# Attention scores for two query tiles at a time, their 64-row rotary products issued in turn on either half of the array's rows

## The chip, the cores and the metric

The kernel runs on one core of a Trainium2 chip. The metric is the device time of one execution in microseconds (us). Engines are named as the profile names them: PE is TensorE's matmul stream, PEld its weight loads, DVE is VectorE, ACT ScalarE, POOL GpSimd, SP SyncE.

## The reference

Two layers of a latent-token backbone, batch 1, 1024 tokens of width 1024, and 256 context tokens. Layer 0 mixes by multi-head latent attention, layer 1 by a Fourier transform. The change is in layer 0's attention. Cut to it:

```
NH, QK_NOPE, QK_ROPE, V_DIM = 8, 128, 64, 128          # 1024 queries, 256 + 1024 keys
k_all = concat([k_ctx, k_lat], axis=1)                 # per head: 128 plain + 64 rotary columns
scale = 1 / sqrt(QK_NOPE + QK_ROPE)
s = einsum('bqhd,bkhd->bhqk', q, k_all) * scale        # the 64 rotary columns of k are shared by all heads
p = softmax(s, axis=-1)
o = einsum('bhqk,bkhd->bqhd', p, v_all)                # then o * silu(gate), output product, residual
```

The low-rank key is used as it stands: the head's key matrix is folded into the query, so that the 128 plain columns of the keys are the same latent vector for all heads, and the head's value matrix is applied behind the sum over keys.

## The kernel before, in words

**Number format.** A float32 product is made from two rounded halves of each factor (`split`: a high part by ACT, the rest by DVE), as high times high, high times low and low times high, each one pass of PE. The probabilities and the latent values are held as two float16 halves each.

**Where the attention lies.** The profiled execution does layer 0's norms, projections and gate until 204.8 us, the attention from 204.8 to 565 us, and layer 0's output product and all of layer 1 behind it. The attention is 8 heads of 8 query tiles of 128; a pair is two neighbouring tiles, 32 in all.

**One tile of scores** (`scores`, L581 to L590) is 128 queries by 1280 keys, in three banks of PSUM, in column pieces of 512, 512 and 256. Five passes go into it. Three are for the plain part: `nkh` with `qh`, `nkl` with `qh`, `nkh` with `ql` (n: keys, q: folded query, h and l: high and low). Two are for the rotary part. `A` holds a head's rotary query, high in rows 0 to 63 and low in rows 64 to 127; `B1` holds the rotary key's low part in rows 0 to 63 and its high part in rows 64 to 127. So `A` with `B1` (128 rows) gives high times low and low times high at once, and high times high is left: `A[0:64]` with `B2` (the key's high part), a product of only 64 rows. That makes 15 matmuls a tile, three of them with 64 rows. Tiles use banks 0 to 2 and 3 to 5 alternately. Banks 6 and 7 are taken in turn by everything else in the attention.

**Behind the scores.** `expo` (L592): DVE takes the row maximum from PSUM (L594), ACT the exponential from PSUM into `p32` with its row sum (L596). This frees the tile's three banks. `quant` (L599): DVE takes the reciprocal and scales it (L600, L602), ACT writes the float16 high part `phi` (L605), DVE the low part `plo` (L607), and each is transposed by a DMA into `PT`. `pv` (L610) is 30 float16 matmuls of 256 columns for a pair, in one bank; `pv_out` splits it into `O` (ACT L90, DVE L91). After each second pair `values` (L619) is three products of `O` with the value matrix in one bank, and DVE multiplies them into `gate` (L623).

**Preparing the next head.** `prep_q` (L559) makes one half of the folded query of head h + 1: the head's weights are split (`wqh`, `wql`), six products go into one bank, and ACT and DVE write `qh` and `ql` from it. `prep_pe` (L570), for two heads at a time and so only during odd heads, transposes the rotary queries into one bank (four transposes) and splits them into two `A`.

**Order.** The loop (L662 to L702) runs over the 64 tiles. `quant` lags the scores by one tile, the product with the values by two pairs (`LAG`), half a pair beside each tile. The order of the instructions on each engine is not written by hand here: a scheduler places them, so `pv`, `values`, `prep_q` and `prep_pe` stand between the passes of the scores. The order of PE is fixed by hand only ahead of the attention.

**Ahead of the attention**, `finish_p2` (L393) transposes a tile of the keys and writes `nkh`, `nkl`, `B1` and `B2`.

Of the kernel before, what the change touches and what calls it, by code (L numbers as in the profile page):

```python
# [17 lines left out]
P = 128  # L18
D = 1024
T = 1024  # L20
# [24 lines left out]
def hybrid_kernel(tc, io, out, dbg=None):  # L45
# [47 lines left out]
    # all of PSUM, handed out bank by bank  # L93
# [69 lines left out]
    # both vectors for a quarter of the array's columns, and the sum over the quarters  # L163
# [98 lines left out]
    def c_mm(k, uc):  # L262
        # one bank holds both: the first write clears it for the two of them
        for t in range(2):
            sl = slice(t * P, (t + 1) * P)
            w = wih[:, k, 256:448], wil[:, k, 256:448]
            for i, (l, r) in enumerate(hl(uc[0][:, sl], uc[1][:, sl], *w)):
                mm(pb[:, 4, t * 192:t * 192 + 192], l, r, start=k + t + i == 0, stop=k == 7 and i == 2, skip_group_check=True)
# [79 lines left out]
    B2 = keyp.tile([64, NC + T], F32R, name="B2")  # L348
# [44 lines left out]
    def finish_p2(nat, t, ctx, kt):  # L393
        tb = bank(7, 1)
        for i in range(2 if ctx else 0, 4):
            nc.tensor.transpose(tb[:, i * P:(i + 1) * P], nat[:, i * P:(i + 1) * P], ident)
        if not ctx:
            dst = slice(t * P, (t + 1) * P)
            split(cqh[:, :, dst], cql[:, :, dst], tb[:, 0:256].rearrange("p (e c) -> p e c", e=2))
        ks = slice(kt * P, (kt + 1) * P)  # L400
        split(nkh[:, ks], nkl[:, ks], tb[:, 256:384])
        act(B1[64:128, ks], tb[64:128, 384:512], AF.Copy)
        split(B2[:, ks], B1[0:64, ks], tb[0:64, 384:512])
# [9 lines left out]
    # a tile's transposes follow two others' arithmetic  # L413
# [21 lines left out]
    # the weights of the rotary queries take a turn among the chunks  # L435
# [33 lines left out]
    def mod_rows(pair):  # L469
        # sums over the partitions, each half of a third in a quarter of the array's columns  # L470
        b = bank(1, 5, 6, 7)
        for c in range(4):
            a = thirds[pair][c // 2][:, (c % 2) * 512:(c % 2) * 512 + 512]
            mm(b[32 * c:32 * c + 32, :], ones[:, 0:32], a, start=True, stop=True)
        row = qmp.tile([P, 512], F32, name="row", tag="row", bufs=1)
        act(row, b, AF.Copy)
        nc.sync.dma_start(modd[2 * pair:2 * pair + 2, :].rearrange("a (h c) -> (a h) c", h=2), row[0:P:32, :])
# [92 lines left out]
    def prep_pe(h, bl):  # L570
        cs = slice(bl * 512, (bl + 1) * 512)
        tb = bank(6, 7)
        for i in range(4):
            nc.tensor.transpose(tb[:, i * P:(i + 1) * P], qpe[:, bl * 4 + i, h * 64:h * 64 + P], ident)  # L574
        for d in range(2):
            A, src = As[(h + d) % 4], tb[64 * d:64 * d + 64, :]
            split(A[0:64, cs], A[64:128, cs], src, scale=SCALE)
# [3 lines left out]
    def scores(h, t):  # L581
        qh, ql = q1[h % 2]
        A1 = As[h % 4]
        s = banks(3, 0, 3).rearrange("p a b -> p (a b)")
        q = slice(t * P, (t + 1) * P)
        passes = [(qh[:, q], nkh), (qh[:, q], nkl), (ql[:, q], nkh), (A1[:, q], B1), (A1[0:64, q], B2)]
        for i, (l, r) in enumerate(passes):
            for a, z in KS:
                mm(s[:, a:z], l, r[:, a:z], start=i == 0, stop=i == 4)  # L589
        return s[:, 0:1280]  # L590
# [39 lines left out]
    s = scores(0, 0)  # L630
    e = expo(s)
# [10 lines left out]
    steps = [(h, t) for h in range(NH) for t in range(8)]  # L642
    PTs, Os, PVb = {}, {}, {}
    prev = None
# [3 lines left out]
    def pv_step(i, half):  # L648
        h, pr = i // 4, i % 4
        if half == 0:  # L650
            PVb[i] = bank(6, 7)
            if pr % 2 == 0:
                Os[h, pr // 2] = [atp.tile([P, 512], F32R, name="O", tag=f"O{j}", bufs=2) for j in range(2)]
            pv(PVb[i], range(0, 5), PTs[i])
        else:
            b = PVb.pop(i)
            pv(b, range(5, 10), PTs.pop(i))
            pv_out(b, pr, Os[h, pr // 2])
            if pr % 2 == 1:
                values(h, pr // 2, Os.pop((h, pr // 2)))  # L660

    for i, (h, t) in enumerate(steps):  # L662
        if t % 2 == 0:
            PTs[i // 2] = [atp.tile([P, 2, NKT, P], F16, name="PT", tag=f"PT{j}", bufs=2) for j in range(2)]
        if i > 0:
            s = scores(h, t)
            e = expo(s)
        if prev is not None:
            quant(*prev)
        prev = (*e, PTs[i // 2], t % 2)  # L670
        if i in (1, 3):
            wvr = atp.tile([P, 4, P], F32, name="wvr", tag="wvr", bufs=1)
            hs = slice(2 * i - 2, 2 * i + 2)
            nc.gpsimd.dma_start(wvr, io["wv"][:, hs, :])
            split(wvh[:, hs, :], wvl[:, hs, :], wvr, scale=gkva)
        if i == 3:
            for n, v in ((2, sh1), (3, scr)):
                nc.gpsimd.dma_start(v, modd[n].rearrange("(k p) -> p k", p=P))
        if i == 16:
            stt(sc1, scr, 1.0, ng[:, 8:16], ALU.add, ALU.mult)  # L680
        if i // 2 >= LAG:
            pv_step(i // 2 - LAG, t % 2)
        if h + 1 < NH:
            if t in (2, 4):
                prep_q(h + 1, t // 2 - 1)
            if h % 2 and t in (3, 5):
                prep_pe(h + 1, t // 4)
        elif t == 0:
# [7 lines left out]
        elif t in (2, 3, 4):  # L696
            k = t - 2
            for i_ in range(2):
                split(*wo0[k][i_], wraw[k][:, i_ * 512:(i_ + 1) * 512], gtt)
        if h == NH - 1 and t in (5, 6, 7):  # L700
            k = t - 1
            nc.gpsimd.dma_start(wraw[k % 4], io["w_out0"][k * P:(k + 1) * P, :])  # L702
# [24 lines left out]
    quant(*prev)  # L727
    for i in (30, 31):
        for half in range(2):
            pv_step(i, half)  # L730
# [168 lines left out]
    # the sum's own token: its products' partial sums are added over the partitions  # L899
# [12 lines left out]
    # odd parts take the place of the input, their weights that of its second half  # L912
# [7 lines left out]
    # projections onto the even halves; the gate's weights make room for them  # L920
# [39 lines left out]
    # the last product's weights: half of the rows early, half in place of the odd parts' weights  # L960
# [292 lines left out]
```

## Time and profile before

| what | value |
|---|---|
| device time, 3 runs | 922.14, 923.68, 926.61 us (median 923.68) |
| span of the profiled execution | 919.9 us, 3.8 below the median of the runs |
| PE busy | 887.2 us, 96% of the span |
| PEld, DVE, ACT, POOL busy | 719.6, 596.9, 407.3, 274.1 us |
| attention, first score product to last product with the values | about 204.8 to 565.1 us |

A busy share near 100% on PE alone does not tell that PE is at its peak, since a matmul's end is modelled; the distance from one matmul's start to the next one's is what a product costs. The other engines' idle time costs nothing as long as PE does not wait for them.

### The profile page before, as it was taken

Reading aid. Unit: us, or ns where it says so; the run is one execution under the profiler, and the core shown is the slowest. Engines: PE = TensorE matmul, PEld = TensorE weight load, DVE = VectorE, ACT = ScalarE, POOL = GpSimd, SP = SyncE. Lnnn points to the kernel's source line nnn. Section 1 sums busy time; section 2 is a strip of 40 time slices with the busy share of each in tenths; the row PEclk is TensorE's granted clock in tenths of the full one; section 3 lists DMA queues with packets and bytes.
Section 4 is the critical chain, followed back from the end, with each engine's and each line's share of the span. In section 5 each row is a group of like instructions: output and inputs, shape, how many; then the busy total and the mean of one; then the engine's idle time right before and its main releaser. Section 6 shows DMA issues by size and latency. Waiting matters only on the chain. (4 is left out here: it accounts for less than half of the span.)

```text
span 919.9 us, 13239 instructions
## 1 busy us (share of the span) xinstructions
PE 887.2 (96%) x4963; PEld 719.6 (78%) x4963; DVE 596.9 (65%) x1058; ACT 407.3 (44%) x697; POOL 274.1 (30%) x242
## 2 busy tenths in 40 slices
PE   4999999989999999999999999999999999999996
PEld 2878877857777777777777777888888889998885
DVE  4366885765777677777677675365288746297654
ACT  4465511136665655655566654223343236332211
POOL 2544362210000000000000504765276635356311
PEclk9999999999999999999999999999999999999999
DMA  8921456723886666566799976312133425642321
GB/s 337 335 87 46 157 165 229 259 86 67 149 138 116 122 120 115 108 122 132 143 167 157 170 138 180 152 69 92 47 137 115 149 92 193 207 132 89 104 87 51
DMA packets 200744, 127.90 MB, mean 139 GB/s; under 512 B 171931, under 2 KB 175708, under 8 KB 200424
## 3 DMA queue, kind: packets, MB, share of 16 engines
q1 hardware_dynamic: 198632, 119.10, 50.0%
q0 software_dynamic: 2048, 7.95, 2.9%
q8 instruction: 39, 0.64, 0.3%
q14 instruction: 25, 0.20, 0.1%
HBM read 72.51 MB, written 12.57 MB: 92 GB/s over the span
## 5 line engine op out<-in xcount | busy, mean ns | idle before, releaser
L596 ACT ACTIVATE p<-pb,mx 128x1280 f32<-128x1280 f32 x64 | 84.9, 1326 | 93.4 <-DVE mx L594 63.9
L594 DVE TENSOR_REDUCE mx<-pb 128x1 f32<-128x1280 f32 x64 | 95.1, 1487 | 38.6 <-PE pb L589 38.5
L607 DVE SCALAR_TENSOR_TENSOR plo<-p,mx,phi 128x1280 f16<-128x1280 f32 x64 | 99.6, 1566 | 25.8 <-ACT phi L605 24.7
L80 PE MATMUL pb<-PT,n16h 128*128 128x256 f16 x640 | 109.3, 274 | 0.0
L589 PE MATMUL pb<-B,A 128*128 128x512 f32 (+3 forms) x384 | 99.5, 374 | 0.0
L605 ACT ACTIVATE phi<-p,mx 128x1280 f16<-128x1280 f32 x64 | 85.9, 1357 | 21.8 <-DMA PT<-phi 10.6
L80 PE MATMUL pb<-PT,n16l 128*128 128x256 f16 x320 | 87.3, 273 | 0.0
L589 PEld LDWEIGHTS pb<-B,A 128*128 128x128 f32 (+1 forms) x384 | 62.4, 186 | 26.1 <-issue 17.5
L695 POOL DMA_DIRECT2D qpe<-w_out x4 | 2.1, 534 | 244.1 <-PE pb L574 244.1
L80 PEld LDWEIGHTS <-n16h 128*128 128x128 f16 x640 | 59.2, 98 | 19.5 <-issue 12.9
L88 POOL TENSOR_TENSOR ol<-gate,oh 128x512 fp32r<-128x512 f32 (+4 forms) x30 | 43.4, 1460 | 64.6 <-ACT oh L87 64.6
L464 DVE SCALAR_TENSOR_TENSOR aacc<-aw,actc,aacc 128x512 f32<-128x512 f32 x49 | 44.3, 922 | 17.7 <-DMA aacc<-b_ada 9.8
L589 PE MATMUL pb<-nkh,qh 128*128 128x512 f32 (+1 forms) x192 | 53.4, 384 | 0.1
L80 PE MATMUL pb<-wl,oh 128*128 128x512 f32 x128 | 50.1, 393 | 1.5 <-DVE wl L88 1.4
L80 PE MATMUL pb<-uh,gh 128*128 128x512 f32 x128 | 50.4, 394 | 0.0
L80 PE MATMUL pb<-ul,gh 128*128 128x512 f32 x128 | 50.1, 392 | 0.0
L80 PE MATMUL pb<-uh,gl 128*128 128x512 f32 x128 | 50.0, 391 | 0.0
L80 PE MATMUL pb<-wh,ol 128*128 128x512 f32 x128 | 49.8, 391 | 0.0
L80 PE MATMUL pb<-wh,oh 128*128 128x512 f32 x128 | 49.0, 397 | 0.0
L589 PE MATMUL pb<-nkl,qh 128*128 128x512 f32 (+1 forms) x192 | 47.9, 357 | 0.0
L589 PE MATMUL pb<-nkh,ql 128*128 128x512 f32 (+1 forms) x192 | 47.8, 357 | 0.0
L87 ACT ACTIVATE oh<-gate 128x512 fp32r<-128x512 f32 (+4 forms) x38 | 19.6, 556 | 54.4 <-PE pb L80 43.9
(327 smaller groups left out, 2204.6 us busy)
## 6 DMA issues: line engine op xcount, KB each, us to landing
aw<-w_ada SPq DMA_DIRECT2D x49, 256.0 KB, 3.4
wada<-wada SPq DMA_DIRECT2D x16, 512.0 KB, 9.1
gr<-wg SPq DMA_DIRECT2D x14, 512.0 KB, 4.1
xn<-x SPq DMA_DIRECT2D x8, 512.0 KB, 5.4
xt<-x SPq DMA_DIRECT2D x8, 512.0 KB, 7.4
h1d<-xt SPq DMA_DIRECT2D x8, 512.0 KB, 2.6
wz<-wz SPq DMA_DIRECT2D x8, 512.0 KB, 4.1
ht<-h1d SPq DMA_DIRECT2D x8, 512.0 KB, 5.4
```

What stands on the lines that cost most here:

```text
L80: mm(ps, l, r, start=start and i == 0, stop=stop and i == n - 1)
L87: act(hi, src, AF.Copy)
L88: eng(lo, src, f32(hi), ALU.subtract)
L464: op = stt(a[:, cs], w, actc[:, k, 0:1], a[:, cs], ALU.mult, ALU.add)
L589: mm(s[:, a:z], l, r[:, a:z], start=i == 0, stop=i == 4)
L594: nc.vector.tensor_reduce(mx[:, 0:1], s, axis=AX, op=ALU.max, negate=True)
L596: act(p32, s, AF.Exp, bias=mx[:, 0:1], accum_out=mx[:, 1:2])
L605: act(hi, p32, AF.Copy, scale=r)
L607: stt(lo, p32, r, hi, ALU.mult, ALU.subtract)
L695: nc.gpsimd.dma_start(wraw[k], io["w_out0"][k * P:(k + 1) * P, :])
```

## The change

The loop runs over the 32 pairs. `scores(h, pr)` makes both tiles of a pair, the even tile in banks 0 to 2, the odd one in banks 3 to 5. First come four passes with 128 rows for the even tile, then four for the odd one. The last of the four is `A` with `B1` for the even tile and `A` with `B2` for the odd one: for odd tiles `A` now holds its low part in rows 0 to 63 and its high part below, and `B2` has 128 rows, the key's high part above and its low part below. So either kind of tile still has one 128-row pass for its two small rotary products, and one product of 64 rows (high times high) left over. Then, for each of the three column pieces, the even tile's 64-row product runs on rows 0 to 63 of the array and the odd tile's on rows 64 to 127, one after the other in program order. The number of matmuls is the same, 30 a pair.

```diff
-    B2 = keyp.tile([64, NC + T], F32R, name="B2")
+    B2 = keyp.tile([P, NC + T], F32R, name="B2")
...
-        act(B1[64:128, ks], tb[64:128, 384:512], AF.Copy)
-        split(B2[:, ks], B1[0:64, ks], tb[0:64, 384:512])
+        split(B1[64:128, ks], B2[64:128, ks], tb[64:128, 384:512])
+        split(B2[0:64, ks], B1[0:64, ks], tb[0:64, 384:512])
...
+        pairs = lambda v, e: v.rearrange("p (a e c) -> p a e c", e=2, c=P)[:, :, e, :]
         for d in range(2):
             A, src = As[(h + d) % 4], tb[64 * d:64 * d + 64, :]
-            split(A[0:64, cs], A[64:128, cs], src, scale=SCALE)
+            for e in range(2):
+                top, low = (pairs(A[64 * x:64 * x + 64, cs], e) for x in range(2))
+                split(*((low, top) if e else (top, low)), pairs(src, e), scale=SCALE)
...
-    def scores(h, t):
+    def scores(h, pr):
         qh, ql = q1[h % 2]
         A1 = As[h % 4]
-        s = banks(3, 0, 3).rearrange("p a b -> p (a b)")
-        q = slice(t * P, (t + 1) * P)
-        passes = [(qh[:, q], nkh), (qh[:, q], nkl), (ql[:, q], nkh), (A1[:, q], B1), (A1[0:64, q], B2)]
-        for i, (l, r) in enumerate(passes):
-            for a, z in KS:
-                mm(s[:, a:z], l, r[:, a:z], start=i == 0, stop=i == 4)
-        return s[:, 0:1280]
+        s = [pb[:, 3 * e:3 * e + 3, :].rearrange("p a b -> p (a b)") for e in range(2)]
+        q = [slice((2 * pr + e) * P, (2 * pr + e + 1) * P) for e in range(2)]
+        for e in range(2):
+            passes = [(qh, nkh), (qh, nkl), (ql, nkh), (A1, B2 if e else B1)]
+            for i, (l, r) in enumerate(passes):
+                for a, z in KS:
+                    mm(s[e][:, a:z], l[:, q[e]], r[:, a:z], start=i == 0, stop=False)
+        for a, z in KS:
+            for e in range(2):
+                x = slice(64 * e, 64 * e + 64)
+                mm(s[e][:, a:z], A1[x, q[e]], (B1 if e else B2)[x, a:z], start=False, stop=True)
+        return [v[:, 0:1280] for v in s]
...
+    order = tc.manual_schedule(engines={mybir.EngineType.PE})
+    order.__enter__()
+    for i in range(4 * NH):
+        h, pr = i // 4, i % 4
...
+            ss = scores(h, pr)
+            es = [expo(s) for s in ss]
+        for e in range(2):
+            quant(*es[e], PTs[i], e)
...
+        if i > LAG:
+            values_step(i - LAG - 1)
         if h + 1 < NH:
-            if t in (2, 4):
-                prep_q(h + 1, t // 2 - 1)
-            if h % 2 and t in (3, 5):
-                prep_pe(h + 1, t // 4)
+            if pr in (1, 2):
+                prep_q(h + 1, pr - 1)
+                if h % 2:
+                    prep_pe(h + 1, pr - 1)
...
+        if i >= LAG:
+            pv_step(i - LAG)
```

Three things come with it. PE's order through the whole loop is now fixed by hand: the pair's scores; `values` of the third pair before, where due; `prep_q` (heads 0 to 6, pairs 1 and 2 of a head); `prep_pe` (odd heads, the same pairs); and last the whole product with the values of the pair two before. There is no second set of banks for the scores: a pair takes all six. And `A` is written in four pieces of 64 by 2 by 128 instead of two of 64 by 512, the keys' rotary part in two splits instead of a copy and a split (ten more DVE operations of 64 by 128 ahead of the attention).

On PE, during head 1, beside the first `prep_pe`, there stood before (qh_2033 and ql_2034 are the head's folded query, B_773 is `B1`, B_774 `B2`):

```order
L589 MATMUL pb<-nkh,qh_2033 128x512 x2
L589 MATMUL pb<-nkh,qh_2033 128x256
L574 MATMUL pb<-ident,qpe 128x128 x4
L589 MATMUL pb<-nkl,qh_2033 128x512 x2
L589 MATMUL pb<-nkl,qh_2033 128x256
L589 MATMUL pb<-nkh,ql_2034 128x512 x2
L589 MATMUL pb<-nkh,ql_2034 128x256
L589 MATMUL pb<-B_773,A_1924 128x512 x2
L589 MATMUL pb<-B_773,A_1924 128x256
L589 MATMUL pb<-B_774,A_1924 128x512 x2
L589 MATMUL pb<-B_774,A_1924 128x256
L589 MATMUL pb<-nkh,qh_2033 128x512 x2
```

With the change, in head 1's pair 2, from the odd tile's last 128-row pass on (L600 are the 64-row products, L575 the transposes of `prep_pe`, O with gh and gl `values`, cq with wq `prep_q`, PT with n16 the product with the values):

```order
L596 MATMUL pb<-B_774,A_1934 128x256
L600 MATMUL pb<-B_774,A_1934 128x512
L600 MATMUL pb<-B_773,A_1934 128x512
L600 MATMUL pb<-B_774,A_1934 128x512
L600 MATMUL pb<-B_773,A_1934 128x512
L600 MATMUL pb<-B_774,A_1934 128x256
L600 MATMUL pb<-B_773,A_1934 128x256
L80 MATMUL pb<-O,gh_781 128x512 x2
L80 MATMUL pb<-O,gl_782 128x512
L80 MATMUL pb<-cqh,wqh 128x512
...
L575 MATMUL pb<-ident,qpe 128x128 x4
L80 LDWEIGHTS n16h
```

The three 64-row products of each tile have become six in a row for a pair, and everything that uses banks 6 and 7 has moved from between the passes to behind the pair's scores, in one order: `values`, `prep_q`, `prep_pe`, product with the values. Counted through the whole program, 70 stretches of 64-row products stood in PE's order before, 36 of them followed by a float32 product and 34 by a float16 one; now there are 32, 23 and 9 of each kind.

On DVE, around the same two halves of `prep_q` and `prep_pe` in head 1, there stood before:

```order
L91 SCALAR_TENSOR_TENSOR ql_1922<-pb,gks,qh_1921 128x512
L594 TENSOR_REDUCE mx<-pb 128x1
L607 SCALAR_TENSOR_TENSOR plo<-p_2442,mx,phi 128x1280
L600 RECIPROCAL mx<-mx 128x1
L602 TENSOR_SCALAR mx<-mx 128x1
L91 SCALAR_TENSOR_TENSOR O<-pb,O 128x256
L91 SCALAR_TENSOR_TENSOR A_2035<-pb,A_2035 64x512
L594 TENSOR_REDUCE mx<-pb 128x1
L607 SCALAR_TENSOR_TENSOR plo<-p_2494,mx,phi 128x1280
L91 SCALAR_TENSOR_TENSOR A_2036<-pb,A_2036 64x512
L600 RECIPROCAL mx<-mx 128x1
L623 TENSOR_TENSOR gate<-pb,gate 128x512
```

With the change, in pair 2 of head 1 (L605 is the maximum, L634 the product with `gate`, L611 and L613 the reciprocal and its scale):

```order
L605 TENSOR_REDUCE mx<-pb 128x1 x2
L634 TENSOR_TENSOR gate<-pb,gate 128x512
L611 RECIPROCAL mx<-mx 128x1
L88 TENSOR_TENSOR wql<-wqk,wqh 128x256
L613 TENSOR_SCALAR mx<-mx 128x1
L91 SCALAR_TENSOR_TENSOR ql_1932<-pb,gks,qh_1931 128x512
L611 RECIPROCAL mx<-mx 128x1
L613 TENSOR_SCALAR mx<-mx 128x1
L618 SCALAR_TENSOR_TENSOR plo<-p_2595,mx,phi 128x1280
L91 SCALAR_TENSOR_TENSOR A_2072<-pb,A_2072 64x2x128
```

Both maxima of a pair stand one behind the other now, and the operations that free banks 6 and 7 (`gate`, `ql`, `A`, `O`) stand behind them. In pair 1 of an odd head `ql` comes directly behind the two maxima.

## Rows read from the trace of the kernel before

**Rows 1.** The page: span, and PE's busy time, share, instructions.
```profile
span 919.9 us, 13239 instructions
PE 887.2 (96%) x4963; PEld 719.6 (78%) x4963; DVE 596.9 (65%) x1058; ACT 407.3 (44%) x697; POOL 274.1 (30%) x242
```
**Rows 2.** Busy time by stretch; the last columns are granted clock, DMA share, GB/s.
```profile
188.40:196.00 7.60, 4.98 (x13) 1.02 (x13) 5.00 (x7) 1.00 (x2) 0.00 (x0) 0.78 0.38 129
235.00:566.00 331.00, 331.00 (x1992) 259.32 (x1991) 232.03 (x316) 190.40 (x252) 18.37 (x20) 1.00 0.74 135
```
**Rows 3.** Timeline of PE, 402 to 404 us: start, length of the group, instruction.
```profile
402.15 0.73 PE L589 MATMUL pb<-nkh,ql 128*128 128x512 f32 x3
402.72 1.54 PE L589 MATMUL pb<-B,A 128*128 128x512 f32 x6
```
**Rows 4.** Timeline of PE, single products of one tile's end, 403.2 to 404.9 us.
```profile
403.20 0.70 PE L589 MATMUL pb<-B,A 128*128 128x256 f32 x2
...
403.41 0.73 PE L589 MATMUL pb<-B,A 64*128 64x512 f32 x2
...
403.74 0.51 PE L589 MATMUL pb<-B,A 64*128 64x512 f32 x2
...
403.98 0.28 PE L589 MATMUL pb<-B,A 64*128 64x256 f32 x1
404.18 0.50 PE L589 MATMUL pb<-nkh,qh 128*128 128x512 f32 x1
...
404.52 0.51 PE L589 MATMUL pb<-nkh,qh 128*128 128x512 f32 x2
```
**Rows 5.** Timeline of PEld, 403.4 to 403.6 us: one load, and two.
```profile
403.40 0.18 PEld L589 LDWEIGHTS pb<-B,A 64*128 64x128 f32 x1 [0.26 <-issue]
...
403.40 0.29 PEld L589 LDWEIGHTS pb<-B,A 64*128 64x128 f32 x2 [0.26 <-issue]
```
**Rows 6.** Timeline of PE: column quarters, and products of 65 rows.
```profile
36.63 1.07 PE L231 MATMUL pb<-wada,act 128*32 128x256 f32 x16
...
799.88 0.28 PE L80 MATMUL pb<-tabx,px 65*128 65x258 f32 x1
800.00 0.28 PE L80 MATMUL pb<-tabh,g1h 128*128 128x256 f32 x1
```
**Rows 7.** Groups by line and shape, 240 to 600 us: busy, mean ns.
```profile
L594 DVE TENSOR_REDUCE mx<-pb 128x1 f32<-128x1280 f32 x58 | 86.2, 1487 | 30.3 <-PE pb L589 30.2
...
L623 DVE TENSOR_TENSOR gate<-pb,gate 128x512 f32<-128x512 f32 x16 | 11.0, 685 | 6.5 <-PE pb L80 6.4
...
L91 DVE SCALAR_TENSOR_TENSOR ql<-pb,gks,qh 128x512 fp32r<-128x512 f32 x12 | 9.0, 749 | 3.6 <-ACT qh L90 3.5
```
**Rows 8.** Timelines of PE, DVE and ACT, 207 to 214 us: the attention's first tiles.
```profile
207.47 1.54 PE L589 MATMUL pb<-B,A 128*128 128x512 f32 x6
...
209.04 1.49 DVE L594 TENSOR_REDUCE mx<-pb 128x1 f32<-128x1280 f32 x1 [1.72 <-PE pb L589]
...
210.57 1.33 ACT L596 ACTIVATE p<-pb,mx 128x1280 f32<-128x1280 f32 x1 [2.83 <-DVE mx L594]
211.80 0.19 ACT L596 ACTIVATION_READ_ACCUMULATOR p<-pb,mx 128x1 f32 x1
212.01 1.28 ACT L491 ACT_TABLE_LOAD   x1
```
**Rows 9.** Timeline of PE, 558.8 to 559.7 us: two key tiles of the values' product.
```profile
559.10 0.38 PE L80 MATMUL pb<-PT,n16h 128*128 128x256 f16 x2
...
559.43 0.38 PE L80 MATMUL pb<-PT,n16h 128*128 128x256 f16 x2
```
**Rows 10.** Timeline of PE, two waits outside the attention.
```profile
192.15 3.37 PE L474 MATMUL pb<-aacc,ones 128*32 128x512 f32 x4 [2.62 <-DVE aacc L464]
...
570.17 0.50 PE L80 MATMUL pb<-wl,oh 128*128 128x512 f32 x1 [1.44 <-DVE wl L88]
570.50 0.39 PE L80 MATMUL pb<-wh,ol 128*128 128x512 f32 x1
```

More of the change, by code (lines that the diff above doesn't have):

```diff
@@ L629, in hybrid_kernel @@
     prep_q(0, 1, bank(5))
-    s = scores(0, 0)
-    e = expo(s)
+    ss = scores(0, 0)
+    es = [expo(s) for s in ss]
     gate_chunk(8, 1)
@@ L641, in hybrid_kernel, with pv_step @@
     wvh, wvl = gws[0]
-    steps = [(h, t) for h in range(NH) for t in range(8)]
     PTs, Os, PVb = {}, {}, {}
-    prev = None
     wo0 = [None] * 8
     wraw = [qpe[:, 2 * i:2 * i + 2, :].rearrange("p a c -> p (a c)") for i in range(4)]
-    def pv_step(i, half):
+    def pv_step(i):
         h, pr = i // 4, i % 4
[L650 to L660, printed above, removed]
@@ L662, in hybrid_kernel @@
-    for i, (h, t) in enumerate(steps):
-        if t % 2 == 0:
-            PTs[i // 2] = [atp.tile([P, 2, NKT, P], F16, name="PT", tag=f"PT{j}", bufs=2) for j in range(2)]
-        if i > 0:
[L666 to L671, printed above, removed]
+        b = bank(6, 7)
+        if pr % 2 == 0:
+            Os[h, pr // 2] = [atp.tile([P, 512], F32R, name="O", tag=f"O{j}", bufs=2) for j in range(2)]
@@ new lines, in pv_step, with values_step @@
+        pv(b, range(10), PTs.pop(i))
+        pv_out(b, pr, Os[h, pr // 2])
+    def values_step(i):
+        h, pr = i // 4, i % 4
+        if pr % 2 == 1:
+            values(h, pr // 2, Os.pop((h, pr // 2)))
+    order = tc.manual_schedule(engines={mybir.EngineType.PE})
+    order.__enter__()
+    for i in range(4 * NH):
+        h, pr = i // 4, i % 4
+        PTs[i] = [atp.tile([P, 2, NKT, P], F16, name="PT", tag=f"PT{j}", bufs=2) for j in range(2)]
+        if i > 0:
+            ss = scores(h, pr)
+            es = [expo(s) for s in ss]
+        for e in range(2):
+            quant(*es[e], PTs[i], e)
+        if i in (0, 1):
@@ L672, in hybrid_kernel @@
             wvr = atp.tile([P, 4, P], F32, name="wvr", tag="wvr", bufs=1)
-            hs = slice(2 * i - 2, 2 * i + 2)
+            hs = slice(4 * i, 4 * i + 4)
             nc.gpsimd.dma_start(wvr, io["wv"][:, hs, :])
             split(wvh[:, hs, :], wvl[:, hs, :], wvr, scale=gkva)
-        if i == 3:
+        if i == 1:
             for n, v in ((2, sh1), (3, scr)):
                 nc.gpsimd.dma_start(v, modd[n].rearrange("(k p) -> p k", p=P))
-        if i == 16:
+        if i == 8:
             stt(sc1, scr, 1.0, ng[:, 8:16], ALU.add, ALU.mult)
-        if i // 2 >= LAG:
-            pv_step(i // 2 - LAG, t % 2)
+        if i > LAG:
+            values_step(i - LAG - 1)
@@ L683, in hybrid_kernel @@
         if h + 1 < NH:
-            if t in (2, 4):
-                prep_q(h + 1, t // 2 - 1)
-            if h % 2 and t in (3, 5):
-                prep_pe(h + 1, t // 4)
-        elif t == 0:
+            if pr in (1, 2):
+                prep_q(h + 1, pr - 1)
+                if h % 2:
+                    prep_pe(h + 1, pr - 1)
+        elif pr == 0:
             close(cq_cm)
@@ L695, in hybrid_kernel @@
                 nc.gpsimd.dma_start(wraw[k], io["w_out0"][k * P:(k + 1) * P, :])
[L696 to L702, printed above, removed]
+        else:
+            for k in ((0,), (1, 2), ())[pr - 1]:
+                for i_ in range(2):
+                    split(*wo0[k][i_], wraw[k][:, i_ * 512:(i_ + 1) * 512], gtt)
+            for k in ((), (4,), (5, 6))[pr - 1]:
+                nc.gpsimd.dma_start(wraw[k % 4], io["w_out0"][k * P:(k + 1) * P, :])
+        if i >= LAG:
+            pv_step(i - LAG)
     ots = [None] * 8
@@ L726, in hybrid_kernel @@
         o_split(t, slice(0, 7), wop, gtt)
-    quant(*prev)
+    values_step(29)
     for i in (30, 31):
-        for half in range(2):
-            pv_step(i, half)
+        pv_step(i)
+    values_step(31)
+    order.__exit__(None, None, None)
     b0 = [pb[:, 0:2, :], pb[:, 2:4, :]]
```

## The prediction

> **What bounds the kernel now.** I read the page first: PE is busy 887.2 of 919.9 us [rows 1]. A busy share over the whole span hides stages, so the table by stretch comes next. In the attention's steady part PE is busy 331.00 of 331.00 us at full granted clock, DVE 232 and ACT 190 [rows 2]. So in this stage only what PE executes counts, and whatever makes PE wait there is new. DVE and ACT have slack on the average, which says nothing about what they owe PE at a given moment.
>
> Then the timeline of PE, since a matmul's length includes its way through the array and only distances between starts are costs. A pass of 512, 512 and 256 columns takes 402.72 - 402.15 = 0.57 us [rows 3]; divided by 2.5 that is 0.23 for 512 columns and 0.117 for 256. A single tile's end shows what the 64-row pass costs more [rows 4]. From the last 128-row product (256 columns) to the first 64-row one 0.21 instead of 0.117: 0.09 lost. From the first to the second 0.33 instead of 0.23: 0.10 lost. On leaving, 403.98 to 404.18 is 0.20 instead of 0.117: 0.08 lost, and if a float32 product follows, its successor starts 0.34 later instead of 0.23: 0.11 lost. Only the change of the array's shape costs this, for a product of 65 rows, run in the full shape, stands at the ordinary 0.12 between its neighbours [rows 6]. The 64-row products themselves gain nothing from using half the rows.
>
> **Switches saved.** 70 stretches of 64-row products become 32 (the order of the program). Entering: 38 x (0.09 + 0.10) = 7.2 us. Leaving: 38 x 0.08 = 3.0. Float32 successors: 36 become 23, 13 x 0.11 = 1.4. Sum 11.6 us.
>
> **Two halves at once.** The six 64-row products of a pair cost 2 x (0.23 + 0.23 + 0.117) = 1.16 us one after the other [rows 3]. Issued in turn on separate halves they can overlap. Nothing before runs on row halves side by side. Column quarters do: 16 products of 256 columns took 1.07 us, 0.07 each instead of 0.117 [rows 6], which is partial overlap of parts of the array. Bounds: no overlap, 0; complete overlap, the six in 0.58, 32 x 0.58 = 18.6 us. In between lie the weight loads: two loads of 64 rows take 0.29 where one takes 0.18, so a load follows a load after 0.11 [rows 5]. If loads go one at a time, the odd half runs 0.11 behind the even one and the six take 0.58 + 0.11 = 0.69; the gain is 0.47 x 32 = 15.1 us. I take this value, because the load row is the nearest one. The page "TensorEngine Tiling (Array Packing)" of the Trainium skill, Key Properties, says that different tiles can load weights and multiply in parallel; by it the six would take 0.58, and no row here shows two loads at once.
>
> Gains together: 26.7 us, bounds 11.6 and 30.2.
>
> **What PE waits for instead.** Call T the start of a pair's last score product. A maximum begins 0.31 us after that: the product that ends at 207.47 + 1.54 = 209.01 is 0.28 long, and the maximum starts at 209.04 [rows 8, 4]. A maximum takes 1.49, and both of a pair now stand in a row on DVE, so they end near T + 3.2. The gate product (0.69) or `ql` (0.75) comes behind them [rows 7]. These free banks 6 and 7, and with three users of two banks behind one pair of scores, the third must wait for the first one's reader.
> - Pair 2 of heads 2, 4, 6: `values`, `prep_q`, then the product with the values in `values`' bank. PE is there at T + 0.2 (leaving) + 3 x 0.23 + 6 x 0.23 + 0.2 (leaving, restart) = T + 2.5; the bank is free when gate is done, T + 3.2 + 0.65 = T + 3.85. Wait 1.3, three times: 3.9 us.
> - Pair 1 of heads 1, 3, 5: `prep_q`, `prep_pe`, product with the values in `prep_q`'s bank. PE is there at T + 0.2 + 1.4 + 0.1 + 0.4 = T + 2.1, `ql` is done at T + 3.85: 1.7. Pair 2 of those heads: `prep_pe` waits for gate (T + 2.5 against T + 3.85: 1.35), and the product with the values for `ql`, which has a reciprocal, `wql` and a scale ahead of it, so another 0.8. Together 3.85 a head: 11.6 us.
> - Start: pair 2 needs the banks of pair 1, and nothing but `prep_q` (1.4 us) lies between, since the first product with the values comes behind pair 2's scores. On ACT, `qh` of that `prep_q` (0.7, done near T + 2.7), then the exponential's table (1.28) and the first exponential (1.33 + 0.19) [rows 8] end at T + 5.5; PE is there at T + 1.6. Wait 3.9 us. The table must come again, because the gate's last chunk lies between two exponentials.
> - Last head, no `prep_q`: the scores of pair 0 and 2 come 0.7 before the exponential, where a `plo` (1.55) is still ahead of the maximum: 1.4 us.
> - Six of these waits stand before a float32 product, which restarts 0.1 late, as the one behind the wait at 570.17 did (its successor is at 570.50): 0.6 us.
> - Before the attention one idle time of 2.62 us was followed by four products that took 3.37 [rows 10], and the granted clock of that stretch is 0.78, against 1.00 in the steady one [rows 2]: (1 - 0.78) x 7.6 = 1.7 us lost. The waits of 1.44 us elsewhere [rows 10] are followed by ordinary distances. The start's 3.9 us are longer than 2.62, so I count 1.7 there and none for the others.
>
> Losses: 3.9 + 11.6 + 3.9 + 1.4 + 0.6 + 1.7 = 23.1 us. Bounds: 17 (start covered by work, no clock loss) and 33 (rival three).
>
> **At no price.** Ten more operations on DVE before the attention and the finer writes of `A` lie beside PE work; without that cover the ten cost some 2 us, but PE waits for `aacc`, a chain through DMA and DVE, at 192 us anyway [rows 10]. In every other pair the product with the values (ten key tiles of 0.33 [rows 9], 3.3 us) covers the way from T to the even tile's exponential: 0.31 + 1.49 + 0.03 + 1.33 + 0.19 = T + 3.4 [rows 8]. This cover is thin: PE arrives at T + 3.5 where neither `values` nor `prep_q` stands.
>
> **Sum.** 26.7 - 23.1 = 3.6 us less. Span 919.9 - 3.6 = 916.3; the profiled execution lies 3.8 below the median of the runs, so 920.1 us. A measurement of this kernel can tell about 0.5% (4.6 us) from no change, so this is on the near side of that line.
>
> **Rivals.**
> - One: both halves load and multiply at once, six products in 0.58, and no clock loss at the start. 3.5 + 1.7 more: 923.7 - 8.8 = 914.9; down to 911 if the start's wait is covered. The load row [rows 5] is against it. The rule of the Trainium skill's tiling page quoted above, loads and products of different tiles in parallel, is for it.
> - Two, the other side: the halves don't overlap. Then only the switches are saved: 11.6 - 23.1 = 11.5 slower, 935.2 us; without the clock's 1.7, 933.5. It decides once the six take over 0.69 + 3.6 / 32 = 0.80 us. For it: no row shows rows in halves. Against it: column quarters [rows 6].
> - Three: all six banks go with one pair, so every pair without `prep_q` depends on the chain of maximum and exponential. If a `plo` stands before the maximum there too, as in the last head, the 14 pairs 0 and 3 of seven heads wait 0.5 more each: 7 us, 927 us. DVE's 232 and ACT's 190 of 331 us [rows 2] speak against it as long as the mean counts, the long chain behind both maxima speaks for it. The Trainium skill's page "TensorEngine Tiling (Array Packing)", PSUM Bottleneck, is on this rival's side: tiling speeds up TensorE but not the emptying of PSUM.
>
> **How the numbers follow.** Forecast 0.36 (917 to 923.5), one 0.24 (911 to 917), three 0.22 (923.5 to 929), two 0.18 (929 to 936). The range 911.5 to 931 leaves out most of two and an edge of one. Faster by over 0.5% (below 919.1): all of one and some of the forecast, 0.39. Within 0.5%: the rest of the forecast and half of three, 0.35. Slower: two and the other part of three, 0.26.
>
> **What would show it.** In the changed profile: the six 64-row products in 0.69 us, starts about 0.11 apart at first (0.58 is rival one, 1.16 rival two); one entry and one exit a pair; PE idle some 21 us in the attention, in the pattern of heads (nothing in pairs 0 and 3, 1.3 in pair 2 of even heads, 1.7 and 2.1 in odd ones), named by gate, `ql` and, once, the exponential; a low granted clock only behind the start. The prediction is wrong if waits show in pairs 0 and 3 too, or if the six take another time than 0.69.

## The result and the profile after

The changed kernel takes 929.46 us (median of 5 runs, 928.76 to 930.69), the kernel before 923.68 (5 runs beside them, 922.14 to 926.61): ratio 1.006, interval 1.0039 to 1.0081. It is 5.8 us slower. The forecast was 3.6 us faster, and "slower" had a chance of 0.26.

The profiled execution has a span of 927.0 us, 7.1 more than [rows 1]. The page gives the span, and PE's busy time with its share and count:

```profile
span 927.0 us, 13296 instructions
PE 865.0 (93%) x4963; PEld 710.3 (77%) x4963; DVE 603.1 (65%) x1084; ACT 406.2 (44%) x713; POOL 273.7 (30%) x242
```

PE executes the same 4963 matmuls in 22.2 us less busy time, and the kernel is slower. So PE now waits, and the first question is where. Three points of PE's timeline cut the span in parts:

| | before | after | difference |
|---|---|---|---|
| first score product | 204.80 | 213.17 | +8.4 |
| first score product to last product with the value matrix (`values`) | 362.60 | 361.64 | -1.0 |
| from there to the end | 352.5 | 352.2 | -0.3 |
| span | 919.9 | 927.0 | +7.1 |

The lines on which the first row rests, before and after:

```profile
204.80 0.74 PE L589 MATMUL pb<-nkh,qh 128*128 128x512 f32 x3
```

```profile
213.17 0.74 PE L596 MATMUL pb<-nkh,qh 128*128 128x512 f32 x3
```

Both kernels execute the same products between the second row's two points. The attention, to which the change was made, is hardly shorter. The loss lies ahead of it, where the forecast counted nothing.

**The six products.** PE's timeline at a place without a wait (start, length of the group, instruction; L596 are the 128-row score products, L600 the 64-row ones):

```profile
401.46 0.74 PE L596 MATMUL pb<-B,A 128*128 128x512 f32 x3
402.13 0.85 PE L600 MATMUL pb<-B,A 64*128 64x512 f32 x6
402.90 0.50 PE L80 MATMUL pb<-cqh,wqh 128*128 128x512 f32 x1
```

From the first of the six to the next full-shape product it is 402.90 - 402.13 = 0.77 us. Before, three products of one tile took 404.18 - 403.41 = 0.77, measured in the same way [rows 4]. Six cost what three cost. A narrower cut of the same timeline, beginning at 402.10, shows the first two lying on each other:

```profile
402.13 0.50 PE L600 MATMUL pb<-B,A 64*128 64x512 f32 x2
```

A single product at such a place is 0.50 long (the one at 404.18 in [rows 4]), and so are these two together. Over all 96 such pairs of the attention the second half's product starts 0 to 15 ns behind the first half's, 3 in the median.

**The waits in the attention.** The view of waits of PE from 225 to 575 us (what waited, for whom; total, times, longest):

```profile
PE pb L596 <- ACT p L607: 8.1, 4, 3.5
PE pb L80 <- DVE ql L91: 6.2, 6, 1.6
PE pb L575 <- DVE gate L634: 4.3, 3, 1.4
PE pb L80 <- DVE gate L634: 3.9, 3, 1.3
PE pb L80 <- DMA PT<-plo: 0.5, 1, 0.5
PE pb L80 <- ACT O L90: 0.5, 1, 0.5
```

18 waits, 23.5 us; the same view of before, from 205 to 567 us, is empty, as PE's 331.00 of 331.00 had said [rows 2]. All but the last two lines are waits for a bank: L607 is the exponential (it frees a pair's scores), `ql` and `gate` free banks 6 and 7. DVE's timeline at the first odd head shows why they are late:

```profile
270.89 2.89 DVE L605 TENSOR_REDUCE mx<-pb 128x1 f32<-128x1280 f32 x2 [0.59 <-PE pb L600]
273.69 0.74 DVE L91 SCALAR_TENSOR_TENSOR ql<-pb,gks,qh 128x512 fp32r<-128x512 f32 x1
```

`ql` stands behind both maxima of the pair and ends 3.54 us after they began.

Measured from start to start, less the distance of the same two kinds of product without a wait, the 18 waits cost 26.7 us: 23.5 idle, and some 0.18 each that the view doesn't count as idle. The busy time by stretch (PE, PEld, DVE, ACT, POOL, then granted clock, DMA share, GB/s) shows a further loss:

```profile
122.00:126.00 4.00, 4.00 (x12) 3.09 (x12) 3.18 (x8) 0.00 (x0) 0.00 (x0) 0.59 0.86 270
235.00:240.00 5.00, 4.95 (x19) 4.15 (x20) 3.19 (x7) 4.42 (x5) 0.00 (x0) 0.71 0.26 42
235.00:566.00 331.00, 311.50 (x1986) 251.53 (x1987) 240.67 (x335) 194.60 (x270) 17.59 (x17) 0.99 0.72 134
374.00:378.00 4.00, 4.00 (x23) 2.95 (x23) 2.63 (x5) 3.45 (x6) 0.00 (x0) 0.57 0.01 2
```

Behind the start's wait the mean granted clock is 0.71 for 5 us: parts of that stretch ran at 1.2 GHz, (1 - 0.71) x 5 = 1.45 us. Behind the waits of one odd head (374 to 378) it is 0.57, and that pair is 15.34 us long where the other odd heads have 13.68: 1.65 us. So PE's own work in the attention is 361.6 - 26.7 - 3.1 = 331.8 us against 362.6, some 30.8 less. This is a difference, not a measurement of its own; the upper bound of the gain was 30.2.

**Ahead of the attention.** PE's timeline (in square brackets the idle time before an instruction and what ended it):

```profile
117.24 0.39 PE L80 MATMUL pb<-uh,gl 128*128 128x512 f32 x1
121.69 0.66 PE L80 MATMUL pb<-gh,cqh 128*128 128x512 f32 x1 [4.06 <-DVE B L88]
122.15 0.63 PE L80 MATMUL pb<-gl,cqh 128*128 128x512 f32 x1
122.57 0.63 PE L80 MATMUL pb<-gh,cql 128*128 128x512 f32 x1
...
200.83 3.22 PE L475 MATMUL pb<-aacc,ones 128*32 128x512 f32 x4 [3.82 <-DVE aacc L465]
```

PE waits 4.06 us for a split of the key's rotary part (L88, tile `B`), and the next products stand 0.42 to 0.46 apart instead of 0.23, at the granted clock of 0.59 in the first row of the table above. DVE's timeline tells why the split is late:

```profile
116.67 0.74 DVE L465 SCALAR_TENSOR_TENSOR aacc<-aw,actc,aacc 128x512 f32<-128x512 f32 x1
117.44 0.29 DVE L88 TENSOR_TENSOR B<-pb,B 64x128 fp32r<-64x128 f32 x1
119.87 1.45 DVE L465 SCALAR_TENSOR_TENSOR aacc<-aw,actc,aacc 128x512 f32<-128x512 f32 x2 [2.13 <-DMA aw<-w_ada]
121.35 0.28 DVE L88 TENSOR_TENSOR B<-pb,B 64x128 fp32r<-64x128 f32 x1
```

There are two splits of `B` for a key tile now. The last one, of 0.28 us, stands behind two sums of `aacc` that wait 2.13 us for a transfer. What the split needs from ACT (L87, 118.16 to 118.42) was done 2.9 us before it starts, but on DVE it comes only behind them, and PE, which needs the bank, waits for the split. In the kernel before the last split and those sums stand the other way round:

```profile
115.40 0.28 DVE L88 TENSOR_TENSOR B<-pb,B 64x128 fp32r<-64x128 f32 x1
117.17 1.42 DVE L464 SCALAR_TENSOR_TENSOR aacc<-aw,actc,aacc 128x512 f32<-128x512 f32 x2 [1.48 <-DMA aw<-w_ada]
```

There the transfer holds up nothing but the sums. How the delay reaches the start is shown by DVE's waits between 105 and 201 us:

```profile
DVE aacc L465 <- POOL aacc L455: 9.8, 1, 9.8
DVE aacc L465 <- DMA aw<-w_ada: 8.7, 6, 3.3
DVE qpe L508 <- PE pb L80: 5.9, 2, 5.4
```

And before, between 105 and 193 us:

```profile
DVE qpe L507 <- PE pb L80: 1.0, 1, 1.0
```

DVE now waits 5.9 us in front of `qpe`, which needs PE's late products; before, 1.0. Behind `qpe` in DVE's order stand the next sums. The first of the 64 sums starts 2.4 us later than before, the 13th 3.0, the 19th 6.7, and the last 8.7. PE waits for the second set of them until 200.83 (192.15 before [rows 10]), 8.7 us later, of which 8.4 are left at the first score product.

### The profile page after: what moved, and what is told of

Same layout as the page of the kernel before. It is cut to its first block, busy times and chain, and to the rows that moved or that the text cites. A ratio compares the mean times of both kernels' runs of the same rounds, so it can differ in the third digit from the quotient of the medians.

```text
span 927.0 us, 13296 instructions
## 1 busy us (share of the span) xinstructions
PE 865.0 (93%) x4963; PEld 710.3 (77%) x4963; DVE 603.1 (65%) x1084; ACT 406.2 (44%) x713; POOL 273.7 (30%) x242
## 5 line engine op out<-in xcount | busy, mean ns | idle before, releaser
L607 ACT ACTIVATE p<-pb,mx 128x1280 f32<-128x1280 f32 x64 | 84.8, 1327 | 93.2 <-DVE mx L605 93.2
L605 DVE TENSOR_REDUCE mx<-pb 128x1 f32<-128x1280 f32 x64 | 92.4, 1485 | 22.8 <-PE pb L600 22.8
L80 PEld LDWEIGHTS <-n16h 128*128 128x128 f16 x640 | 61.5, 99 | 26.0 <-issue 18.2
L88 POOL TENSOR_TENSOR ol<-gate,oh 128x512 fp32r<-128x512 f32 (+4 forms) x30 | 42.8, 1441 | 70.1 <-ACT oh L87 70.1
L596 PE MATMUL pb<-nkh,qh 128*128 128x512 f32 (+1 forms) x192 | 50.9, 373 | 8.1 <-ACT p L607 8.1
L465 DVE SCALAR_TENSOR_TENSOR aacc<-aw,actc,aacc 128x512 f32<-128x512 f32 x49 | 42.0, 877 | 19.0 <-POOL aacc L455 9.8
L596 PE MATMUL pb<-nkl,qh 128*128 128x512 f32 (+1 forms) x192 | 48.2, 359 | 0.0
L596 PE MATMUL pb<-nkh,ql 128*128 128x512 f32 (+1 forms) x192 | 47.9, 358 | 0.0
L596 PE MATMUL pb<-B,A 128*128 128x512 f32 (+1 forms) x192 | 47.6, 356 | 0.0
L596 PEld LDWEIGHTS pb<-nkh,qh 128*128 128x128 f32 x192 | 32.0, 191 | 14.1 <-ACT p L607 9.4
L87 ACT ACTIVATE oh<-gate 128x512 fp32r<-128x512 f32 (+4 forms) x38 | 19.6, 556 | 52.3 <-PE pb L80 42.9
```

The costliest lines, as they stand in the source:

```text
L80: mm(ps, l, r, start=start and i == 0, stop=stop and i == n - 1)
L87: act(hi, src, AF.Copy)
L88: eng(lo, src, f32(hi), ALU.subtract)
L465: op = stt(a[:, cs], w, actc[:, k, 0:1], a[:, cs], ALU.mult, ALU.add)
L596: mm(s[e][:, a:z], l[:, q[e]], r[:, a:z], start=i == 0, stop=False)
L605: nc.vector.tensor_reduce(mx[:, 0:1], s, axis=AX, op=ALU.max, negate=True)
```

## The experiments

**1. The key splits alone.** The kernel before, with only the additional key splits (the lower half of `B2` is written and not read).

```diff
-    B2 = keyp.tile([64, NC + T], F32R, name="B2")
+    B2 = keyp.tile([P, NC + T], F32R, name="B2")
...
-        act(B1[64:128, ks], tb[64:128, 384:512], AF.Copy)
-        split(B2[:, ks], B1[0:64, ks], tb[0:64, 384:512])
+        split(B1[64:128, ks], B2[64:128, ks], tb[64:128, 384:512])
+        split(B2[0:64, ks], B1[0:64, ks], tb[0:64, 384:512])
```

> The kernel before with one part of the change alone: the keys' rotary part is written by two splits instead of a copy and a split, and the added lower half of B2 is not used. Attention as before. Theory one (the ten more DVE operations come before the sums for the conditioning on DVE and make PE wait at the rotary queries, and the whole chain up to the attention moves): the attention begins near 213 us instead of 204.8, the time is 932, between 929 and 934. Theory two (the later start comes from the loop's new order or the new writing of A, not from the key splits): 923.7, within 1.5.

Measured: 930.62 us (929.49 to 933.30), ratio 1.0081 (1.0062 to 1.0100). This preparation alone costs 930.62 - 923.37 = 7.25 us, and PE's timeline has the same wait:

```profile
123.05 0.80 PE L80 MATMUL pb<-gh,cqh 128*128 128x512 f32 x1 [4.83 <-DVE B L88]
...
213.84 0.74 PE L589 MATMUL pb<-nkh,qh 128*128 128x512 f32 x3
```

The whole loss of the change, and a little more, is in a part that the forecast put at nothing. What the attention gives back is the difference to the full change, 930.62 - 929.46 = 1.2 us (1.9 by the two ratios), near the 1.0 of the table above.

**2. The key's low part by a transfer.** The changed kernel, with the copy of before on ACT, and one transfer that copies `B2`'s upper half into its lower one.

```diff
-        split(B1[64:128, ks], B2[64:128, ks], tb[64:128, 384:512])
+        act(B1[64:128, ks], tb[64:128, 384:512], AF.Copy)
...
     turn_p(1)
+    nc.gpsimd.dma_start(B2[64:128, :], B1[0:64, :])
     close(pt_cm)
```

> The changed kernel, with the lower half of B2 brought by one DMA from the upper half of B1 instead of ten more splits. Theory one: the attention begins near 204.8 again, the waits within it stay, the time is 929.5 - 8.4 = 921, between 919.5 and 922.5. Theory two (the start is late for another reason): 929.5.

Measured: 920.30 us (917.41 to 923.57), ratio 0.9966 (0.9950 to 0.9982), a time as expected. The waits in the attention are those of the changed kernel (22.6 us in all). PE's wait at the place in question is 0.97 us, the first score product starts at 208.87 (expected near 204.8; the two profiles of before have 204.80 and 207.50), and the kernel is 929.46 - 920.30 = 9.2 us faster than the change as it was made. (The profiled execution is this kernel's longest, 923.57 us.) So the DVE operations ahead of the attention, and not the wider tile or the attention's new order, turned a gain into a loss.

**3. The halves not in turn.** The even tile's three 64-row products first, then the odd tile's three.

```diff
-        for a, z in KS:
-            for e in range(2):
+        for e in range(2):
+            for a, z in KS:
```

> The changed kernel, but of the six 64-row products of a pair the even tile's three come first, then the odd tile's three; same halves, same data. If halves run at once only where neighbours in the order are on different halves, the six take 0.23 x 4 + 0.117 = 1.04 us instead of 0.58, and those parts that PE did not wait for behind it show: 32 x 0.46 = 14.7 at most, some of it absorbed by the waits (no: these count from the last score product) so 944, between 940 and 945. If the order does not matter (each half has its own queue), 929.5.

Measured: 933.46 us (930.57 to 936.49), ratio 1.0110 (1.0089 to 1.0131): neither theory. PE's timeline says that the order in the program doesn't decide the overlap:

```profile
404.55 0.85 PE L600 MATMUL pb<-B,A 64*128 64x512 f32 x6
405.32 0.51 PE L80 MATMUL pb<-cqh,wqh 128*128 128x512 f32 x1
```

0.77 again. The six start in three pairs, each second one 3 to 22 ns behind the first, 10 in the median. The trace doesn't name the half, but on one half starts are 0.12 us apart and more (experiment 5), so the odd half's first product starts with the even half's first, though two others stand ahead of it in the program. The 4.0 us come from DVE, where the scheduler put a reciprocal and its scale (L611, L613) between the maxima and `ql`:

```profile
269.91 2.89 DVE L605 TENSOR_REDUCE mx<-pb 128x1 f32<-128x1280 f32 x2 [0.45 <-PE pb L600]
272.94 0.16 DVE L611 RECIPROCAL mx<-mx 128x1 f32<-128x1 f32 x1
273.14 0.15 DVE L613 TENSOR_SCALAR mx<-mx 128x1 f32<-128x1 f32 x1
273.52 0.75 DVE L91 SCALAR_TENSOR_TENSOR ql<-pb,gks,qh 128x512 fp32r<-128x512 f32 x1 [0.23 <-ACT qh L90]
```

PE's longest wait for `ql` grows from 1.6 to 2.4 us, and behind it the granted clock is low, in each of the three odd heads:

```profile
274.30:278.00 3.70, 3.67 (x19) 2.65 (x19) 2.36 (x5) 3.65 (x5) 0.00 (x0) 0.54 0.00 0
```

These pairs are 14.98 us long against 12.49 in the changed kernel, 3 x 2.49 = 7.5 us in the profiled execution; its attention is 368.1 us long, 6.5 more.

**4. The product with the values first.** `pv_step` ahead of `values`, `prep_q` and `prep_pe`, so that its 3.3 us lie between a pair's last score product and the first user of banks 6 and 7.

```diff
+        if i >= LAG:
+            pv_step(i - LAG)
         if i > LAG:
             values_step(i - LAG - 1)
...
-        if i >= LAG:
-            pv_step(i - LAG)
```

> The changed kernel, with the product with the values of the pair two before moved ahead of values, prep_q and prep_pe in PE's order of each pair; the banks 6 and 7 are then taken in that order. Theory one (the waits in the attention are for banks 6 and 7, whose readers gate and ql stand behind both maxima on DVE): the waits of 1.8, 1.6 + 0.7 and 1.5 us (16.6 in all) fall to some 6, since 3.3 us of products now lie ahead of the first operation that needs the bank again: 929.5 - 10 = 919.5, between 916 and 923. Rival (the waits only move to O, whose split is late on DVE as well): 927 to 931.

Measured: 923.44 us (922.23 to 925.58), ratio 0.9999 (0.9988 to 1.0011), 6.0 us faster than the changed kernel and just outside of what was expected. PE's waits in the attention:

```profile
PE pb L596 <- ACT p L607: 6.2, 2, 3.5
PE pb L80 <- DVE A L91: 5.9, 3, 2.0
PE pb L80 <- DVE mx L613: 3.5, 3, 1.2
PE pb L80 <- DMA PT<-plo: 1.4, 1, 1.4
PE pb L575 <- DVE O L91: 1.4, 3, 0.5
```

The waits for `ql` and `gate` are gone. In their place stand waits for the splits of `A` (the rotary query of the next two heads), which DVE does behind the next pair's maxima, and three of 1.2 us in heads 2, 4 and 6. The attention is 355.9 us long, 5.7 less than the changed kernel's; the start is as late as ever (214.34).

**5. Both tiles on the same half.** The changed kernel's order, with both tiles' 64-row products on rows 0 to 63; the key splits of before suffice for it, and `A` is laid out as before.

```diff
-                x = slice(64 * e, 64 * e + 64)
-                mm(s[e][:, a:z], A1[x, q[e]], (B1 if e else B2)[x, a:z], start=False, stop=True)
+                mm(s[e][:, a:z], A1[0:64, q[e]], B2[:, a:z], start=False, stop=True)
```

> The changed kernel's loop, order and banks, but the 64-row products of both tiles of a pair on rows 0 to 63, with the keys' and the queries' halves laid out as before (so no added splits of the keys). Theory one: nothing overlaps, the six take 1.16 us instead of 0.58, 32 x 0.58 = 18.6 us more in the attention than in the changed kernel, and the start of the attention is back near 205 (8.4 less): 929.5 + 18.6 - 8.4 = 939.7, between 937 and 942. Rival (two tiles side by side save mostly by fewer changes of the array's shape, and overlap is worth little): 921 to 925.

Measured: 936.17 us (934.19 to 940.22), ratio 1.0145 (1.0124 to 1.0165), a little less than expected. PE's timeline:

```profile
415.56 1.42 PE L599 MATMUL pb<-B,A 64*128 64x512 f32 x6
416.92 0.73 PE L80 MATMUL pb<-O,gh 128*128 128x512 f32 x2
```

On one half the six take 416.92 - 415.56 = 1.36 us, on two 0.77: the halves are worth 0.59 a pair, 18.9 us for the 32 pairs. Its attention is 13.4 us longer than the changed kernel's (375.0 against 361.6), not 18.9. PE's waits there add up to 19.3 us instead of 23.5: what PE does longer, it waits less, and none of its odd heads has the low clock's 1.65 us. This kernel is also rival two at work: only the switches saved, and the waits.

**6. The sums behind the splits.** The first set of sums, `at(0)`, moved behind the last two calls that prepare the keys.

```diff
-    at(0)
     gate_w0(1)
...
     turn_p(1)
+    at(0)
     close(pt_cm)
```

> The changed kernel, with the first sums for the conditioning placed behind the last two tiles of keys in the program instead of ahead of them, so that the last key splits on DVE no longer stand behind sums that wait for their weights. Theory one (PE waits 4.06 us at 117 us for the last split, and runs 1.6 us slower at a low clock behind it, because of that order): the wait is gone and with it some 5 of the 8.4 us: 924.5, between 922.5 and 926. Rival (the sums, begun later, move the second set of sums at 192 us by as much, so nothing is won): 928 to 931.

Measured: 925.70 us (924.13 to 930.30), ratio 1.0030 (1.0017 to 1.0043). The time is in the expected range, the way to it is not. PE's timeline:

```profile
117.43 0.39 PE L80 MATMUL pb<-gh,cqh 128*128 128x512 f32 x1
...
162.95 1.91 PE L475 MATMUL pb<-aacc,ones 128*32 128x512 f32 x2 [5.28 <-DVE aacc L465]
...
211.94 0.74 PE L596 MATMUL pb<-nkh,qh 128*128 128x512 f32 x3
```

The wait for the split is gone, as meant. But the first of the sums now starts at 115.23 instead of 107.63, and PE waits for the first set of them instead, so that the attention starts only 1.2 us earlier; the kernel is 3.8 us faster than the changed one (2.8 by the two ratios), and still slower than the kernel before. The two chains, PE's and that of the sums, are both near the path here: it helps little to take one out of the other's way, as long as it starts late itself.

**7. Both mended.** Experiments 2 and 4 together, the transfer a little later, behind all `q_rope` calls.

```diff
     for t in range(4, 8):
         q_rope(2, t)
+    nc.gpsimd.dma_start(B2[64:128, :], B1[0:64, :])
...
+        if i >= LAG:
+            pv_step(i - LAG)
         if i > LAG:
             values_step(i - LAG - 1)
```

> The changed kernel with both remedies: the lower half of B2 by one DMA, now issued only behind the rotary queries (where the DMA engines are little used), and the product with the values ahead of values, prep_q and prep_pe. Theory one (the two losses are independent and add up): 920.3 of the DMA alone, less some 1 for its later place, less the 5.7 that the attention became shorter by the other order: 913.5, between 912 and 915.5. Rival (the gains overlap, since the attention's start and its waits share one chain): 917 to 921.

Measured: 915.68 us (913.51 to 920.60), ratio 0.9918 (0.9900 to 0.9935): 7.6 us faster than the kernel before, and better than experiments 2 and 4 alone. That is 0.2 above the range of the theory that both gains add up, and 1.3 below that of its rival. It starts the attention at 208.61.

**8. The start's wait filled.** Experiment 7 with 14 products more in pair 1 that write an unused bank and that nobody reads, at the place where PE waits for the first exponential.

```diff
+        if i == 1:
+            b = bank(6, 7)
+            for _ in range(14):
+                mm(b, q1[0][0][:, 0:P], nkh[:, 0:512], start=True, stop=True)
```

> As both remedies together, with 14 useless products of 512 columns into a free bank behind pair 1's prep_q, where PE otherwise waits 3.7 us for the exponential. Theory (an idle PE of that length is granted a low clock for the next 3 us or so, which costs 1.4 us): the wait is filled, no work becomes shorter, but the granted clock behind it stays at 1.00, 1.4 us less than with both remedies: 912. Rival (the low clock has another cause, or the products delay pair 2 as much): equal to both remedies or up to 1 slower.

Measured: 916.37 us (912.24 to 918.07), ratio 0.9917 (0.9898 to 0.9935), not to be told from experiment 7. The stretch in question did what was expected. The busy times behind the start's wait, of experiment 7:

```profile
230.50:234.00 3.50, 3.47 (x12) 2.86 (x13) 1.71 (x6) 3.50 (x5) 0.00 (x0) 0.64 0.10 23
```

and with the wait filled:

```profile
230.50:234.00 3.50, 3.50 (x18) 2.97 (x19) 1.71 (x6) 3.50 (x5) 0.00 (x0) 1.00 0.09 21
```

18 products instead of 12 in the same 3.5 us, at 2.4 GHz throughout. From pair 1's first 64-row product to pair 2's it is 10.83 us instead of 12.39, so the low clock behind the start costs 1.56. The runs don't show it: this kernel's runs lie 5.8 us apart, those of experiment 7 7.1, more than the effect.

**9 and 10. Both kernels once more**, for the spread of the start.

> The kernel before once more, for one look at how much the attention's start moves between executions. If the start is fixed by the program, the first score product is at 204.8 again within 0.5; if the loads of the conditioning's weights decide, it moves by a few us, and with it the 2.3 us by which kernels without any added key split still begin later.

> The changed kernel once more, for the same: the first score product within 0.5 of 213.2 if the program fixes it; otherwise some us beside it. The wait of 4 us at 117 us is there in either case, and the waits in the attention are the same; a stretch of low clock may fall behind another one of the odd heads' waits.

One run of each, 924.45 and 928.26 us. The first score product of before starts at 207.50 (204.80 in the first profile), that of the change at 212.73 (213.17). The start itself moves by 2.7 us between executions of the same kernel, so the change's delay is 6.8 us in the mean of two pairs (8.4 and 5.2). PE's wait for the split is there again, 3.61 us at 120.66, and so are 17 of the 18 waits of the attention to 0.2 us. With the attention's -1.0 and -1.2 and the rest's -0.3 and -0.2 the spans of the two pairs differ by 7.1 and 3.8 us, 5.4 in the mean, against 5.8 in the result. In all twelve profiles the two kinds lie apart: the six of kernels with two splits on DVE for a key tile start the attention at 211.9 to 214.3 us, the six with one at 204.8 to 208.9.

## Why the prediction was wrong

**The step that failed** is "At no price. Ten more operations on DVE before the attention [...] lie beside PE work". The prediction named a cover, PE's wait for `aacc` at 192 us, and called it "a chain through DMA and DVE". That is where it went wrong: the ten operations stand on DVE, in that chain. A cover that ends when DVE is done can't hide what DVE does more. Nor were "some 2 us" the price without a cover; the runs showed 6.8 us in its place. That the splits are the cause is shown by experiments 1 and 2. The traces say that not their 10 x 0.28 us of work cost most, but the place of one: behind two sums that wait for a transfer it holds up PE by 4.06 us; a low clock follows, then DVE's wait for PE's late products, then the sums. In both pairs of profiles the delay of the sums grows by 3.7 us between the 13th and the 19th, where that wait of DVE stands, and by 2.0 and 1.9 behind it. What the 13th has already differs, 3.0 us in the first pair and 0.2 in the second. This way is read from the traces, not shown by a run: experiment 6 broke its first link and met another wait, so what each link alone costs stays open.

**The gain was forecast too small.** The switches were taken at 11.6 us and the halves at 15.1, on the assumption that loads go one at a time and six products take 0.69. They take 0.58 beside the switches, 18.6 us; with the switches that makes 30.2, and 30.8 came out as a difference, where 26.7 were forecast. Experiment 5 gives the halves alone 18.9. The load row [rows 5] was the wrong neighbour: its two loads go to the same half. The page "TensorEngine Tiling (Array Packing)" of the Trainium skill, Key Properties, says that different tiles load weights and multiply in parallel; the trace agrees, with six products in 0.77 us where three had 0.77. This was rival one's mechanism.

**The waits came nearly as forecast**, by place and by releaser:

| wait | forecast | measured (from start to start) |
|---|---|---|
| pair 2 of heads 2, 4, 6, for `gate` | 3.9 | 4.4 |
| pairs 1 and 2 of heads 1, 3, 5, for `ql` and `gate` | 11.6 | 11.9 |
| start, for the exponential | 3.9 | 3.7 |
| last head | 1.4 | 6.7 |
| low clock behind the start | 1.7 | 1.5 |
| low clock behind an odd head's waits | 0 | 1.7 |

The 0.6 us for late restarts were not measured apart. Two terms were mis-sized, the last head and, smaller, the low clock, which came once more than counted. In the last head five waits stand, not two: three for the exponential (5.3 us), one for a transposed probability and one for ACT's part of an `O`. The two that the forecast counted had 0.7 each; the three are 1.6 to 2.0 each. The forecast had one `plo` (1.55 us) ahead of the maxima there. DVE's timeline has two in a row, 3.0 us, ahead of the second of these waits:

```profile
522.44 3.02 DVE L618 SCALAR_TENSOR_TENSOR plo<-p,mx,phi 128x1280 f16<-128x1280 f32 x2 [4.02 <-DMA PT<-plo]
525.37 2.88 DVE L605 TENSOR_REDUCE mx<-pb 128x1 f32<-128x1280 f32 x2
```

They begin only when a transfer has landed, for which DVE waits 4.02 us. Two also stand ahead of the maxima of the other two waits. No run tried another order there. In the rest of the attention pairs 0 and 3 have no wait at all, as forecast, so rival three, which wanted one in each of them, did not come about.

In sum the attention was forecast at -26.7 + 23.1 = -3.6 us and is -30.8 + 29.8 = -1.0. That these errors nearly cancel is luck. The sign of the result comes from the failed step alone: without its 6.8 us the change would be some 1 us faster, and with the preparation on ACT and a transfer it is 3.1 us faster (experiment 2); where the other 2 us come from is open. That the time lies within 911.5 to 931 is luck too: the upper part of that range was for rivals two and three, and neither came about. The bound of 33 us for the losses, called rival three's, doesn't follow from its own 7 us either: 23.1 + 7 is 30.1.

**Rival two** was wrong as a forecast and right in its price: with both tiles on one half, experiment 5 is 12.9 us slower than before, where the rival gave 11.5 for its loop.

## What to carry to other kernels

A short operation is costed by its place, too: look at what stands ahead of it on its engine, above all operations that wait for transfers, and at who waits for it. A wait for an engine is no cover for work added to that same engine. And where two independent tiles are made to finish together, PE's gain is paid back at the banks: put PE's longest independent block (here the product with the values) directly behind the pair, before anything that needs a bank the other engines still hold, which was worth 6.0 us on the changed kernel, and 4.6 from experiment 2 to experiment 7, where the transfer also moved.

## What the runs showed of the hardware

- The two row halves work independently of the program's order: with three products of one half ahead of three of the other (experiment 3), the products start in pairs, 10 ns apart in the median, and the six take 0.77 us, as when they are issued in turn. The Trainium skill, page "TensorE: Matmul & The Clock Gate", Part 3 on packing small matmuls, gives starts about 4 ns apart for products in separate row groups; in the changed kernel's trace they are 0 to 15 ns apart, 3 in the median, which agrees.
- The low clock is not the same in each execution. Behind the waits of 3.5 to 3.6 us at the attention's start and of 3.3 to 4.8 us for the last key split the granted clock was low in each profile that has them (0.59 and 0.71 above). Behind the two waits of 1.4 and 0.5 us in an odd head's pair 2 it fell in one of the three heads in both profiles of the change, in another one in experiment 2 and in none in experiment 6; behind one wait of 2.4 us (experiment 3, pair 1) in each of the three. Where one such fall was measured, it cost 1.56 (experiment 8) and 1.65 us. This may be a part of why the runs of experiments 7 and 8 lie 7.1 and 5.8 us apart and those of the kernel before beside them 4.4; that is not shown.
